# RoPE over eight slabs: one load for slabs 2 and 3, one store for slabs 4 and 5

## The chip, the cores and the metric

The kernel runs on one core of a Trainium2 chip. The metric is device time in microseconds: 162.28 us before the change (median of 3 runs, 162.27 to 162.35). The core has a vector engine (DVE), a scalar engine (ACT), a tensor engine (PE), GpSimd (POOL) and SyncE (SP), and 16 DMA engines that move data between the device's memory (DRAM in the names) and the on-chip memory of 128 partitions.

## The reference

`x` holds 16 batches of 512 positions with 1024 values each, 16 heads of 64. In each head the first 32 values and the last 32 values are rotated against each other by an angle of the position:

```python
x = x.reshape(batch, seq, num_heads, head_dim)      # 16, 512, 16, 64
x1, x2 = x[..., :half_dim], x[..., half_dim:]
cos = cos[None, :, None, :]                         # 512 x 32
sin = sin[None, :, None, :]
rotated = np.concatenate([x1 * cos - x2 * sin,
                          x1 * sin + x2 * cos], axis=-1)
```

Input and output are float32, 33.55 MB each.

## The kernel before, in words

**Slabs.** Two batches make a slab (`nb = 2`), so there are eight slabs, 0 to 7, of 4.19 MB. A slab lies in a tile of 128 partitions by 8192 floats (32 KB a partition); a partition holds 8 consecutive positions of one batch, and partitions follow each other in DRAM without gaps. Six slabs fit at a time: the pool `slabs` has six buffers, and slabs 6 and 7 reuse the buffers of slabs 0 and 1.

**Tables.** The cos and sin tables are loaded by two small transfers (line 70), cast to bfloat16 by POOL (line 89), spread over the partitions by four matmuls (line 94) and copied from there by DVE to `tab` (line 100). DVE needs `tab` before its first product.

**The work on a slab** is done in place. ACT casts the float32 values to bfloat16 into the first half of the same bytes (`cast`, line 119). DVE makes two products, with the cos table into the second half and with the sin table onto the first (line 129), and one sum of them with the 32-value halves of each head swapped (line 132). ACT casts the sum back to float32 over the slab (the write-back, line 135). Slabs 1 to 5 are done in one pass of 8192 values a partition, slabs 0, 6 and 7 in two passes of 4096.

**Order.** The loop over passes (line 123) is unrolled. ACT's program runs one pass ahead with its casts: it has the cast of the next pass before the write-back of this one. A scheduler places the instructions on each engine, so a store need not stand right behind its write-back. Each engine takes its instructions in that order and a waiting instruction holds up those behind it. SyncE issues the loads (line 61) and ACT the stores (line 137), each on a DMA queue of its own; both queues are worked off by the same 16 DMA engines. Loads 0 to 5 are issued at the start; load 6 waits for store 0 to have landed, and load 7 for store 1, since they go to the same buffers. Each transfer reports to one of eight semaphores, which are dealt out in turn, so that a transfer can also come to wait for an earlier one that uses the same semaphore.

Of the kernel before, what the change touches and what calls it, by code (L numbers as in the profile page):

```python
# [2 lines left out]

# [4 lines left out]


@with_exitstack  # L10
def kernel(
    ctx: ExitStack,
    tc: tile.TileContext,
    x: bass.AP,
    cos: bass.AP,
    sin: bass.AP,
    num_heads: int,
    out: bass.AP,
):
    nc = tc.nc  # L20
    P = nc.NUM_PARTITIONS

    batch, seq, dim = x.shape
    nh = num_heads
    hd = dim // nh
    half = hd // 2
    bf16 = mybir.dt.bfloat16
    f32 = mybir.dt.float32

    nb = 2  # L30
    slots = 6
    nslabs = batch // nb
    rpp = nb * seq // P
    W = rpp * dim
    SP = seq // rpp
    TW = rpp * half

    out_flat = out.rearrange("b s h d -> b s (h d)")

    singles = ctx.enter_context(tc.tile_pool(name="singles", bufs=1))  # L40
    slabs = ctx.enter_context(tc.tile_pool(name="slabs", bufs=slots))
    psum = ctx.enter_context(tc.tile_pool(
        name="psum", bufs=1, space=bass.MemoryType.PSUM))


    def dram(t, s, a=0, n=W):
        return bass.AP(tensor=t.tensor, offset=t.offset + s * nb * seq * dim + a,
                       ap=[[W, P], [1, n]])


    def view(t, offset, *dims):
        return dataclasses.replace(t, offset=t.offset + offset,
                                   ap=[t.ap[0], *[list(d) for d in dims]])


    slab = {}


    def load(s):
        slab[s] = slabs.tile([P, W], f32, tag="slab", name="slab")  # L60
        nc.sync.dma_start(out=slab[s], in_=dram(x, s))  # L61


    load(0)


    cos_sb = singles.tile([SP, TW], f32, tag="cos_sb")
    sin_sb = singles.tile([SP, TW], f32, tag="sin_sb")
    for t, src in ((cos_sb, cos), (sin_sb, sin)):
        nc.scalar.dma_start(out=t, in_=bass.AP(  # L70
            tensor=src.tensor, offset=src.offset, ap=[[TW, SP], [1, TW]]))

    for s in range(1, slots):
        load(s)

    pick = singles.tile([SP, 2 * P], bf16, tag="pick")
    nc.gpsimd.memset(pick, 0.0)  # L79
    for g in range(2):  # L80
        part = view(pick, g * P, (SP, P // SP), (1, SP))
        nc.gpsimd.affine_select(  # L82
            out=part, in_=part, compare_op=mybir.AluOpType.not_equal,
            fill=1.0 - 2.0 * g, base=0, pattern=[[0, P // SP], [-1, SP]],
            channel_multiplier=1)

    tab1 = singles.tile([SP, 2 * TW], bf16, tag="tab1")
    for i, t in enumerate((cos_sb, sin_sb)):
        nc.gpsimd.tensor_copy(out=view(tab1, i * TW, (1, TW)), in_=t)  # L89

    acc = psum.tile([P, 2 * rpp * hd], f32, tag="acc")
    for i in range(2):
        for h in range(2):
            nc.tensor.matmul(  # L94
                view(acc, i * rpp * hd + h * half, (hd, rpp), (1, half)),
                view(pick, i * h * P, (1, P)),
                view(tab1, i * TW, (half, rpp), (1, half)),
                start=True, stop=True)
    tab = singles.tile([P, 2 * rpp * hd], bf16, tag="tab")
    nc.vector.tensor_copy(out=tab, in_=acc)  # L100

    passes = []
    for s in range(nslabs):
        n = rpp if 1 <= s < nslabs - 2 else rpp // 2
        passes += [(s, r, n) for r in range(0, rpp, n)]


    def halves(u):
        s, r, n = u
        t = slab[s].bitcast(bf16)
        return [view(t, (2 * r + i * n) * dim, (1, n * dim)) for i in range(2)]


    def cast(u):
        s, r, n = u
        nc.scalar.copy(out=halves(u)[0], in_=view(slab[s], r * dim, (1, n * dim)))  # L119


    cast(passes[0])
    for i, u in enumerate(passes):
        s, r, n = u
        if i + 1 < len(passes):
            cast(passes[i + 1])
        lo, up = halves(u)
        for t, a in ((up, 0), (lo, rpp * hd)):
            nc.vector.tensor_mul(  # L129
                out=t, in0=lo,  # L130
                in1=view(tab, a + r * hd, (hd, n), (0, nh), (1, hd)))
        nc.vector.tensor_add(  # L132
            out=up, in0=up, in1=view(lo, half, (hd, n * nh), (-half, 2), (1, half)))

        nc.scalar.copy(out=view(slab[s], r * dim, (1, n * dim)), in_=up)  # L135
        if r + n == rpp:
            nc.scalar.dma_start(out=dram(out_flat, s), in_=slab[s])
            if s + slots < nslabs:
                load(s + slots)


# [1 line left out]
_INS = ['x', 'cos', 'sin', 'num_heads']  # L143
_OUTS = [((16, 512, 16, 64), 'float32')]

_NUMBERS = {'num_heads': 16}


# [26 lines left out]
```

## Time and profile before

| what | us |
|---|---|
| median of 3 runs | 162.28 |
| profiled execution, its own time | 162.04 |
| profiled execution, span | 160.3 |
| ACT busy | 113.3 |
| DVE busy | 108.4 |
| PE busy | 1.2 |

The span runs from the first to the last instruction of the profiled execution; its own time is 1.74 us longer. The busy times are of the span. In the lines with 40 digits every digit is the busy share of one fortieth of the span (4.0 us) in tenths, 9 for 90% or more. In the lines of queues stand packets, MB and the share of the time of all 16 DMA engines that the queue's packets took; `q1` is the loads' queue, `q10` that of the tables and the stores. In the timeline a row is start, duration, engine and line, operation and tiles, and in square brackets the idle time before it and what ended it. `ACTq` and `SPq` are the issuing of transfers by these engines. Rows of waits give the total in us, how many, and the longest.

### The profile page before, as it was taken

How to read it: one execution, taken by the hardware profiler on the slowest of the kernel's cores; microseconds unless marked ns; L12 is line 12 of the kernel's file. 1: busy time of each engine (PE TensorE's matmuls, PEld its weight loads, DVE VectorE, ACT ScalarE, POOL GpSimd, SP SyncE). 2: the span in 40 equal slices, each digit the busy share in tenths (PEclk: the TensorE clock that was granted, in tenths of full speed). 3: DMA queues.
4: the chain of work that ended last, by engine and by line, in shares of the span. 5: the costliest groups of instructions: out<-in, count | busy, mean ns of one | idle time of the engine just before them, and what ended most of it. 6: DMA issues, size and time to landing. Idle time of an engine off the chain costs nothing.

```text
span 160.3 us, 155 instructions
## 1 busy us (share of the span) xinstructions
PE 1.2 (1%) x4; PEld 0.5 (0%) x4; DVE 108.4 (68%) x34; ACT 113.3 (71%) x23; POOL 1.8 (1%) x9
## 2 busy tenths in 40 slices
PE   0001100000000000000000000000000000000000
PEld 0000000000000000000000000000000000000000
DVE  0000399999999998998999199939559499910000
ACT  3005929999949999999939995199995999280000
POOL 2000000000000000000000000000000000000000
DMA  7999999999999999999999999999999999999993
GB/s 245 417 401 409 393 450 458 401 409 491 409 393 499 417 393 466 433 409 450 450 409 401 499 409 393 499 417 393 491 417 401 466 433 409 417 483 409 401 499 147
DMA packets 2465, 67.24 MB, mean 420 GB/s; under 512 B 289, under 2 KB 417, under 8 KB 417
## 3 DMA queue, kind: packets, MB, share of 16 engines
q1 hardware_dynamic: 1152, 33.55, 49.3%
q10 hardware_dynamic: 1312, 33.69, 48.7%
q14 instruction: 1, 0.00, 0.0%
HBM read 33.69 MB, written 33.55 MB: 420 GB/s over the span
## 4 chain that ended last, share of the span: by engine, by line
DMA 50%; DVE 20%; ACT 12%; issue 6%; PE 0%; POOLq 0%; POOL 0%; DVEq 0%; ACTq 0%; SPq 0%
DMA slab<-in_x_dram 27%; DMA out_dram<-slab 16%; DVE slab L129 14%; ACT slab L135 9%; DMA cos_sb<-in_cos_dram 7%; DVE slab L132 6%; ACT slab L119 3%; DVE tab L100 1%; PE acc L94 0%; POOLq L170 0%; POOL tab L89 0%; DVEq L129 0%; SPq L61 0%; ACTq L135 0%; ACTq L119 0%
## 5 line engine op out<-in xcount | busy, mean ns | idle before, releaser
L129 DVE TENSOR_TENSOR slab<-slab,tab 128x4096 bf16<-128x4096 bf16 (+1 forms) x22 | 71.6, 3260 | 13.2 <-ACT slab L119 12.7
L119 ACT CAST slab<-slab 128x4096 bf16<-128x4096 f32 (+1 forms) x11 | 56.6, 5154 | 23.4 <-DMA slab<-in_x_dram 23.4
L135 ACT CAST slab<-slab 128x4096 f32<-128x4096 bf16 (+1 forms) x11 | 56.6, 5154 | 5.7 <-DVE slab L132 5.7
L132 DVE TENSOR_TENSOR slab<-slab 128x4096 bf16<-128x4096 bf16 (+1 forms) x11 | 35.9, 3261 | 0.3
L100 DVE CAST tab<-acc 128x1024 bf16<-128x1024 f32 x1 | 1.2, 1225 | 18.8 <-PE acc L94 18.8
L119 ACT ACT_TABLE_LOAD x1 | 1.3, 1283 | 2.0 <-issue 2.0
L94 PE MATMUL acc<-tab,pick 64*128 64x256 bf16 x4 | 1.2, 392 | 17.6 <-POOL tab L89 17.6
L82 POOL TENSOR_SCALAR_AFFINE_SELECT pick<-pick 64x128 bf16<-64x128 bf16 x2 | 0.5, 286 | 0.1
L89 POOL CAST tab<-cos_sb 64x256 bf16<-64x256 f32 x1 | 0.4, 389 | 10.7 <-DMA cos_sb<-in_cos_dram 10.7
L94 PEld LDWEIGHTS <-pick 64*128 64x128 bf16 x4 | 0.5, 112 | 17.8 <-issue 16.3
L89 POOL CAST tab<-sin_sb 64x256 bf16<-64x256 f32 x1 | 0.4, 394 | 5.0 <-DMA sin_sb<-in_sin_dram 5.0
L79 POOL MEMSET pick<- 64x256 bf16 x1 | 0.3, 304 | 0.3 <-POOLq L156 0.3
L156 POOL MEMSET const-bfloat16-1.0<- 128x1 bf16 x1 | 0.1, 106 | 0.0
L156 POOL MEMSET const-uint8-127<- 128x1 uint8 x1 | 0.1, 106 | 0.0
L156 POOL MEMSET const-float32-0.0<- 128x1 f32 x1 | 0.1, 103 | 0.2 <-issue 0.2
L156 POOL MEMSET const-float32-1.0<- 128x1 f32 x1 | 0.1, 103 | 0.0
## 6 DMA issues: line engine op xcount, KB each, us to landing
slab<-in_x_dram SPq DMA_DIRECT2D x8, 4096.0 KB, 42.6
out_dram<-slab ACTq DMA_DIRECT2D x8, 4096.0 KB, 26.0
cos_sb<-in_cos_dram ACTq DMA_DIRECT2D x1, 64.0 KB, 11.6
sin_sb<-in_sin_dram ACTq DMA_DIRECT2D x1, 64.0 KB, 16.3
```

What stands on the lines that cost most here:

```text
L79: nc.gpsimd.memset(pick, 0.0)
L82: nc.gpsimd.affine_select(out=part, in_=part, compare_op=mybir.AluOpType.not_equal, fill=1.0 - 2.0 * g, base=0, pattern=[[0, P // SP], [-1 ...
L89: nc.gpsimd.tensor_copy(out=view(tab1, i * TW, (1, TW)), in_=t)
L94: nc.tensor.matmul(view(acc, i * rpp * hd + h * half, (hd, rpp), (1, half)), view(pick, i * h * P, (1, P)), view(tab1, i * TW, (half, rpp) ...
L100: nc.vector.tensor_copy(out=tab, in_=acc)
L119: nc.scalar.copy(out=halves(u)[0], in_=view(slab[s], r * dim, (1, n * dim)))
L129: nc.vector.tensor_mul(out=t, in0=lo, in1=view(tab, a + r * hd, (hd, n), (0, nh), (1, hd)))
L132: nc.vector.tensor_add(out=up, in0=up, in1=view(lo, half, (hd, n * nh), (-half, 2), (1, half)))
L135: nc.scalar.copy(out=view(slab[s], r * dim, (1, n * dim)), in_=up)
L156: nc = _bacc.Bacc("TRN2", target_bir_lowering=False, num_devices=1)
```

## The change

Slabs 2 and 3 now lie side by side in one tile of 128 partitions by 16384 floats, and slabs 4 and 5 in another. The pool of single slabs has two buffers in place of six and a new pool `pairs` has two of double size, so the bytes are the same. Slabs 2 and 3 are loaded by one transfer, with each partition's two runs of 32 KB taken from two places 4 MB apart in DRAM; slabs 4 and 5 are still loaded by one transfer each. Slabs 4 and 5 are stored by one transfer, issued when both are done; slabs 2 and 3 are still stored by one each. Sixteen transfers remain of eighteen. Loads 6 and 7 reuse the buffers of slabs 0 and 1 as before.

```diff
-    slabs = ctx.enter_context(tc.tile_pool(name="slabs", bufs=slots))
+    slabs = ctx.enter_context(tc.tile_pool(name="slabs", bufs=2))
+    pairs = ctx.enter_context(tc.tile_pool(name="pairs", bufs=2))
...
+    def both(t, s):
+        return bass.AP(tensor=t.tensor, offset=t.offset + s * nb * seq * dim,
+                       ap=[[W, P], [nb * seq * dim, 2], [1, W]])
...
+    def place(s):
+        t = pairs.tile([P, 2 * W], f32, tag="pair", name="pair")
+        slab[s], slab[s + 1] = view(t, 0, (1, W)), view(t, W, (1, W))
+        return view(t, 0, (W, 2), (1, W))
...
-    for s in range(1, slots):
-        load(s)
-
+    load(1)
+    nc.sync.dma_start(out=place(2), in_=both(x, 2))
+    pair = place(4)
+    for s in (4, 5):
+        nc.sync.dma_start(out=slab[s], in_=dram(x, s))
...
         if r + n == rpp:
-            nc.scalar.dma_start(out=dram(out_flat, s), in_=slab[s])
-            if s + slots < nslabs:
-                load(s + slots)
+            if s == 5:
+                nc.scalar.dma_start(out=both(out_flat, 4), in_=pair)
+            elif s != 4:
+                nc.scalar.dma_start(out=dram(out_flat, s), in_=slab[s])
+            if s < 2:
+                load(s + 6)
```

On ACT the instructions keep their order but for the stores: the store of slab 0 stood behind the cast of slab 2 and now stands before it, and the merged store stands behind the cast of the first and second half of slab 6.

More of the change, by code (lines that the diff above doesn't have):

```diff
@@ L30 @@
     nb = 2
-    slots = 6
     nslabs = batch // nb
@@ L112, in halves @@
         s, r, n = u
-        t = slab[s].bitcast(bf16)
+        t = view(slab[s], 0, (1, W)).bitcast(bf16)
         return [view(t, (2 * r + i * n) * dim, (1, n * dim)) for i in range(2)]
```

## The prediction

> **What bounds the kernel now.** I read the slices of the span first, then the queues, then the stages, the chain of waits and the timeline. The page:
>
> ```profile
> span 160.3 us, 155 instructions
> DVE  0000399999999998998999199939559499910000
> ACT  3005929999949999999939995199995999280000
> DMA  7999999999999999999999999999999999999993
> q1 hardware_dynamic: 1152, 33.55, 49.3%
> q10 hardware_dynamic: 1312, 33.69, 48.7%
> ```
>
> See that both compute engines have holes and the transfers have none: every slice but the first and the last is 9. The two queues (q1 carries the loads that SP issues, q10 the stores and the two tables that ACT issues) took 49.3 + 48.7 = 98.0% of the sixteen engines' time, so 2.0% of 160.3, or 3.2 us, is idle. Is any of that in the middle? The table by stage (after the engines' busy times, the last three columns are the granted clock, the DMA share and GB/s) says no:
>
> ```profile
> 0.00:4.00 4.00, 0.00 (x0) 0.10 (x1) 0.00 (x0) 1.28 (x1) 1.04 (x7) 1.00 0.72 246
> 24.00:38.00 14.00, 0.00 (x0) 0.00 (x0) 13.95 (x6) 14.00 (x4) 0.00 (x0) 1.00 1.01 435
> 38.00:62.00 24.00, 0.00 (x0) 0.00 (x0) 23.12 (x6) 21.76 (x4) 0.00 (x0) 1.00 1.01 436
> 122.00:140.00 18.00, 0.00 (x0) 0.00 (x0) 15.72 (x8) 14.22 (x4) 0.00 (x0) 1.00 1.01 435
> 140.00:157.00 17.00, 0.00 (x0) 0.00 (x0) 0.72 (x1) 3.60 (x1) 0.00 (x0) 1.00 1.00 432
> 157.00:160.30 3.30, 0.00 (x0) 0.00 (x0) 0.00 (x0) 0.00 (x0) 0.00 (x0) 1.00 0.37 159
> ```
>
> The first 4 us miss 28% (1.1 us) and the last 3.3 us miss 63% (2.1 us): together 3.2 us, all the idle time there is. And the rate is the same with loads alone (24 to 38: 435 GB/s), loads beside stores (38 to 62: 436) and stores alone (122 to 157: 435 and 432). So the end is set by bytes: eight slabs of 4.19 MB in and eight out through one full pipe, 9.66 us for each of the sixteen (the last four stores land at 130.33, 140.00, 149.66 and 159.32 by the trace's record of landings). Who issues what when doesn't matter as long as the pipe always has something queued. The prediction is therefore a search for a moment when, after the change, both queues are empty.
>
> The rows of the timeline that the change touches, and SP's waits:
>
> ```profile
> 37.69 7.01 ACT L119 CAST slab<-slab 128x8192 bf16<-128x8192 f32 x1
> 37.81 0.35 ACTq L137 DMA_DIRECT2D out_dram<-slab  x1
> 46.94 7.02 ACT L135 CAST slab<-slab 128x8192 f32<-128x8192 bf16 x1 [2.24 <-DVE slab L132]
> 53.99 0.34 ACTq L137 DMA_DIRECT2D out_dram<-slab  x1
> 103.71 0.34 ACTq L137 DMA_DIRECT2D out_dram<-slab  x1
> 114.26 0.34 ACTq L137 DMA_DIRECT2D out_dram<-slab  x1
> 144.44 0.34 ACTq L137 DMA_DIRECT2D out_dram<-slab  x1
> ```
>
> ```profile
> SPq L61 <- DMA out_dram<-slab: 62.3, 2, 43.3
> SPq L61 <- DMA cos_sb<-in_cos_dram: 9.0, 1, 9.0
> ```
>
> These are the cast of slab 2 (37.69), the issues of stores 0 and 1 (37.81, 53.99), the write-back of slab 1, and the issues of stores 4, 5 and 7. SP's first row is loads 6 and 7 waiting for stores 0 and 1 to land; the second is load 5 waiting for the cos table, with which it shares a semaphore.
>
> **The change, part by part.**
>
> Two transfers removed. Bytes, partitions and 32 KB runs stay as they are. What a boundary between transfers costs is read where one queue runs alone: landings 9.67, 9.66 and 9.66 us apart at 432 to 435 GB/s, with no idle time in the stage. A completion write is 9 ns in the trace's packet records; two fewer on every engine is 0.02 us. The other bound is the load-only stage, where landings are 9.96 and 9.72 us apart (13.81, 23.77, 33.49), 0.30 and 0.06 over the store pitch; if all of that were boundary, two boundaries would give back 0.1 to 0.6 us. I take 0.02, because the store rows are clean of anything else, while in the first load interval the sin table is also moving. The Trainium skill, DMA: Bandwidth & Descriptors, section Anatomy of one DMA, gives every transfer (there issued by GpSimd) a fixed cost of about 2 us beside bytes over the rate; were that paid here in series, two fewer would save 4 us and end near 158.3, but the landings 9.66 us apart have no room for it.
>
> The load of slabs 2 and 3. Slab 2 can no longer be cast when its own bytes are in (33.49, landing record) but when both are. The same bytes are in front of that moment as in front of load 3's landing before, 45.67. So the cast of 2 moves from 37.69 to 45.7. The issue of store 0 stood behind that cast in ACT's program and now stands before it: it stays at 37.8. Behind the cast on ACT stand the write-back of 1, the cast of 3 and the issue of store 1; on DVE the products of 2 wait for it; on SP load 7 waits for store 1. ACT then runs back to back, a full pass every 6.92 us (46.94, 53.86, 60.78, 67.70 in the timeline): cast 2 at 45.7, write-back 1 at 52.6, cast 3 at 59.5, store 1 issued at 59.7 (5.7 us later than before), write-back 2 at 66.4, cast 4 at 73.4, store 2 at 73.5, write-back 3 at 80.3, cast 5 at 87.2, store 3 at 87.3, write-back 4 at 94.1. DVE keeps up: two products and the sum take 13.33 us (46.82 to 60.15), against 13.84 for a cast and a write-back.
>
> Does the pipe run dry here? Store 0's packets end at 59.5. A store issued into a busy pipe sends its first packet 3.6 us later (37.81 to 41.39 for store 0), so store 1 starts near 63.3 and the store queue is empty for 3.8 us. Loads 4 and 5 are queued and take the whole pipe meanwhile: cost 0. They are the cover; without them it would be 3.8 us. Loads then run 1.9 us ahead and stores 1.9 us behind (half of the 3.8). Store 1 lands near 82.5 instead of 80.4 and releases load 7, which is needed only when load 6 is through, near 100: cost 0. Load 5's wait for the cos table goes, and SP's queue issues it some 9 us sooner; the bytes in front of it last past 60, so gain 0.
>
> One store for slabs 4 and 5. The issues at 103.71 and 114.26 become one. Cast 5 ends at 94.2; DVE ends slab 5 at 107.6; its write-back runs 107.6 to 114.7 (the cast of the first half of 6, due when load 6 lands near 101.8, is over by 105.5); the store is issued at 114.7, first packet near 118.3. It stands on ACT behind the cast of 6's second half (114.6) and in front of the write-back of 6's first half (118.2), so its wait holds nothing up. When is it needed? The last packet of all ended at 158.99; four stores of 9.66 from there back give 120.3, the moment when the other twelve slabs are through. Slack 2.0 us, cover: the tails of store 3 and load 7. Cost 0.
>
> The tail. From write-back 5 by the half passes (3.60 and 2.29 us rows): casts and write-backs of 6 and 7 put store 6 at 128.9 (needed by about 136, that is 139.7 less 3.6) and store 7 at 142.8, earlier than 144.44 before since load 7 lands about 2 us earlier; needed by 145.8. Cost 0.
>
> Sharing and rate of the new shape. No row shows a transfer whose engine alternates between two places 4 MB apart. Nearest rows: loads beside stores, where every engine alternates between two tensors, at 436 GB/s (cost 0); the load-only pitch, 0.06 to 0.30 us a slab over the store pitch, which on four slabs is +0.24 to +1.2 us; on the gain side nothing below 9.66 was seen. I take 0, by the mixed row. A rule speaks against the change: the same page, Latency and other measured facts, gives 103 GB/s for partitions laid 4 MiB apart; at that rate the 16.8 MB of the two pairs would take 163 us instead of 39 and the kernel 286 us. Here the partitions stay 32 KB apart and only the two halves are 4 MB apart, so I don't expect it, and no run shown has that layout.
>
> Sum against the profiled execution: 160.3 - 0.02 = 160.3 span, 162.04 with the 1.74 that lies around it. The median shown is 162.28, 0.24 over that execution, so 162.26 there.
>
> **The rivals.**
>
> Slower, the pipe dries up at 120.3. The merged store reaches the engines after loads 0 to 7 and stores 0 to 3 are through. It decides from 2.0 us of lateness on, one for one. The pair could land later than 45.67 if store 0 shared the pipe from the end of its issue (38.2) instead of from 41.39: then 43.1 (23.77 + 2 x 9.67) plus 4.9 us, 48.0, 2.4 late, price 0.4: 162.7. For it: the slack is thin and ACT has no hole between 45.7 and 101. Against: the 41.39 is measured in the same state, and ACT's durations don't vary.
>
> Slower, the pairs' packets run at the load-only pitch or the like: +0.24 to +1.2, 162.5 to 163.5. For it: engines with no spare time, so that 1% on four slabs is already 0.4 us. Against: 435 GB/s in every mix.
>
> Faster, the boundary costs something after all: 0.1 to 0.6, 161.7 to 162.2. For it: 9.96 and 9.72 between the loads. Against: the tail stores.
>
> The change doing nothing of what it says would be a transfer split up again on its way to the queues; the built program has one instruction for each pair, and split ones would give the same 162.3 anyway.
>
> **How the numbers follow.** About 0.2% (0.3 us) is what a measurement of this kernel can tell from no change. Forecast, no change, 162.26: 0.58. Dry pipe 0.10, slower packets 0.18, other losses in a pipe that forgives nothing 0.02: slower 0.30. Cheaper boundaries: 0.12. The range 161.8 to 163.4 takes in most of the boundary gain, the dry pipe and nearly all of the packet price; the likeliest case alone is 162.1 to 162.5.
>
> **What would show it.** Right: 9 in every inner slice of the DMA row; the cast of slab 2 near 45.7; stores 0 and 1 issued near 37.8 and 59.7; the merged store near 114.7; one store queue gap near 60 with loads filling it; the last stores 9.66 us apart. Wrong: a slice under 9 near 120 (dry pipe), the pair landing clearly after 46 or a stage under 430 GB/s where a pair moves (packets), or a span shorter with the same 98% (boundaries).

## The result, and the profile after

The changed kernel takes 164.13 us (median of 22 runs, 162.01 to 165.23), the kernel before beside it 162.25 us (median of 22). The ratio is 1.0056, 95% interval 1.0036 to 1.0076. That ratio leaves out every run more than 1.5% above the fastest of its kernel, and 10 of the changed kernel's own 22 runs lie there, so its median tells more than the ratio. The kernel before keeps within 0.4 us apart from a few runs far off, the changed one spreads over 3.2 us. It is slower, and the forecast of no change was wrong.

The page of the changed kernel, its execution of 165.23 us:

```profile
span 163.4 us, 153 instructions
DVE  0000399999950999899899989999096799600000
DMA  7999999999999999999999899999999899999970
q1 hardware_dynamic: 1136, 33.55, 48.5%
q10 hardware_dynamic: 1296, 33.69, 47.9%
```

The bytes are those of before, and the DMA row is still full but for two 8s, near 92 and 129 us. The last two slices are new: 7 and 0, where before there was one 3. The span is 3.1 us longer, and nearly all transfers are over some 4 us before its end.

The rows of its timeline that answer to those of before (the cast of slab 2, the write-back of slab 1, the issues of stores 0 and 1, the merged store, stores 6 and 7):

```profile
38.08 0.35 ACTq L155 DMA_DIRECT2D out_dram<-slab  x1
45.91 7.02 ACT L134 CAST pair<-pair 128x8192 bf16<-128x8192 f32 x1 [7.86 <-DMA pair<-in_x_dram]
52.83 7.01 ACT L150 CAST slab<-slab 128x8192 f32<-128x8192 bf16 x1
59.88 0.34 ACTq L155 DMA_DIRECT2D out_dram<-slab  x1
114.96 0.39 ACTq L153 DMA_DIRECT2D out_dram<-pair  x1
131.16 0.35 ACTq L155 DMA_DIRECT2D out_dram<-slab  x1
145.33 0.34 ACTq L155 DMA_DIRECT2D out_dram<-slab  x1
```

Up to the merged store these rows are where the prediction put them, to within 0.3 us: cast 45.91 (45.7), store 1 59.88 (59.7), merged store 114.96 (114.7). Stores 6 and 7 are later than worked out, 131.16 against 128.9 and 145.33 against 142.8. That was the first thing to look at, but the next two fences show that it is not the cause. They are tables by stage (the last three columns are granted clock, DMA share and GB/s), first of the changed kernel, then of the kernel before:

```profile
75.00:97.00 22.00, 0.00 (x0) 0.00 (x0) 20.90 (x6) 22.00 (x4) 0.00 (x0) 1.00 1.01 436
97.00:109.00 12.00, 0.00 (x0) 0.00 (x0) 11.93 (x4) 9.06 (x3) 0.00 (x0) 1.00 0.98 412
142.00:158.00 16.00, 0.00 (x0) 0.00 (x0) 0.00 (x0) 3.30 (x1) 0.00 (x0) 1.00 1.01 438
158.00:163.40 5.40, 0.00 (x0) 0.00 (x0) 0.00 (x0) 0.00 (x0) 0.00 (x0) 1.00 0.06 24
```

```profile
97.00:109.00 12.00, 0.00 (x0) 0.00 (x0) 9.37 (x3) 6.58 (x3) 0.00 (x0) 1.00 1.01 434
109.00:122.00 13.00, 0.00 (x0) 0.00 (x0) 9.41 (x5) 12.25 (x3) 0.00 (x0) 1.00 0.96 413
142.00:158.00 16.00, 0.00 (x0) 0.00 (x0) 0.00 (x0) 2.41 (x1) 0.00 (x0) 1.00 0.99 428
158.00:163.40 5.40, 0.00 (x0) 0.00 (x0) 0.00 (x0) 0.00 (x0) 0.00 (x0) 1.00 0.00 0
```

From 142 to 158 us the engines are full in both: store 7 was in time. From 158 us on the changed kernel still moves something, at a share of 0.06. That can be about one engine of sixteen (1/16 = 0.0625) all the time, or many for a moment. From 97 to 109 us it moves 412 GB/s where the kernel before moves 434, at a share that is still 0.98. A full share at a lower rate would mean that the packets take longer, but in so short a stage the rate alone is only a hint: the kernel before also has a stage at 413, with its share down at 0.96. Packets have to decide both questions. This is the view of the transfers, cut to 158 to 163 us:

```profile
DMA  6000060000000060000000006000000000000000
DMA packets 20, 0.13 MB, mean 26 GB/s; under 512 B 16, under 2 KB 16, under 8 KB 16
q10 hardware_dynamic: 20, 0.13, 6.2%
```

Sixteen of these twenty packets are the 4-byte completion writes, one from each engine. The other four are 32 KB stores (0.13 MB). The trace's records of single packets go one step further. They don't name the engine, but a packet starts where the one before it on its engine ended, so the records fall into sixteen chains of 64 loads and 64 stores. Three of the four stores follow each other on one chain, from 158.65 us on, and end at 162.28. A 32 KB packet takes 1.213 us in the median of both kernels. In the kernel before none between 75 and 120 us takes over 1.25 us; in the changed one 33 do, up to 1.82 us, 7.3 us too long in all. They come in bursts near 82 and 99 to 105 us and, on that one engine, at every store from 90 to 117 us: 11 slow packets, 3.1 of the 7.3 us. Of the sixteen completion writes of the last store, fifteen lie between 158.7 and 159.3 us and one at 162.29. So most of the loss is one engine that was slowed by some 3 us while loads and stores ran beside each other, and everybody waits for it at the end.

### The profile page after: what moved, and what is told of

It is laid out like the page before. It is cut to its first block, busy times and chain, and to the rows that moved or that the text cites. A ratio compares the mean times of both kernels' runs of the same rounds, so it can differ in the third digit from the quotient of the medians.

```text
span 163.4 us, 153 instructions
## 1 busy us (share of the span) xinstructions
PE 1.2 (1%) x4; PEld 0.5 (0%) x4; DVE 108.4 (66%) x34; ACT 113.4 (69%) x23; POOL 1.8 (1%) x9
## 4 chain that ended last, share of the span: by engine, by line
DMA 66%; ACT 13%; issue 5%; DVE 4%; SPq 0%; ACTq 0%
DMA pair<-in_x_dram 27%; DMA slab<-in_x_dram 25%; DMA out_dram<-slab 14%; ACT slab L150 9%; ACT slab L134 3%; DVE slab L144 3%; DVE slab L147 1%; ACT pair L134 1%; SPq L68 0%; ACTq L150 0%; ACTq L134 0%
## 5 line engine op out<-in xcount | busy, mean ns | idle before, releaser
L134 ACT CAST slab<-slab 128x4096 bf16<-128x4096 f32 (+1 forms) x7 | 28.5, 4091 | 17.3 <-DMA slab<-in_x_dram 17.3
L144 DVE TENSOR_TENSOR slab<-slab,tab 128x4096 bf16<-128x4096 bf16 (+1 forms) x14 | 36.2, 2595 | 6.4 <-ACT slab L134 6.0
L144 DVE TENSOR_TENSOR pair<-pair,tab 128x8192 bf16<-128x8192 bf16 x8 | 35.4, 4425 | 7.4 <-ACT pair L134 7.3
L134 ACT CAST pair<-pair 128x8192 bf16<-128x8192 f32 x4 | 28.1, 7015 | 7.9 <-DMA pair<-in_x_dram 7.9
L150 ACT CAST slab<-slab 128x4096 f32<-128x4096 bf16 (+1 forms) x7 | 28.5, 4089 | 3.5 <-DVE slab L147 3.5
L150 ACT CAST pair<-pair 128x8192 f32<-128x8192 bf16 x4 | 28.1, 7016 | 1.3 <-DVE pair L147 1.3
L147 DVE TENSOR_TENSOR slab<-slab 128x4096 bf16<-128x4096 bf16 (+1 forms) x7 | 18.2, 2596 | 0.2
L147 DVE TENSOR_TENSOR pair<-pair 128x8192 bf16<-128x8192 bf16 x4 | 17.7, 4425 | 0.1
```

The lines of the kernel that those rows point to most:

```text
L144: nc.vector.tensor_mul(out=t, in0=lo, in1=view(tab, a + r * hd, (hd, n), (0, nh), (1, hd)))
L147: nc.vector.tensor_add(out=up, in0=up, in1=view(lo, half, (hd, n * nh), (-half, 2), (1, half)))
```

## The experiments

**What could slow packets long after the merged load is over?** Three theories. "Late cast": the cast of slab 2 at 45.9 us makes store 1 late, the store queue has a hole near 60 us, and after it loads and stores stand in another lag to each other, in which packets are slowed. "Two places": the merged load upsets the engines. "Merged store": the other half of the change. The first four kernels take the change apart.

The changed kernel once more:

> The changed kernel once more, as the control for the three beside it. All theories: 162 to 165 us, spread over the runs, with one or more of the sixteen DMA engines ending 1 to 3 us after the rest.

162.96 us (median of 12, 161.89 to 165.13), ratio 1.0024, interval 1.0005 to 1.0042. The spread is there again. The profiled execution of this run took 162.37 us, and its slow packets add up to 7.2 us, as many as in the execution of 165.23 us. But here the sum is spread over the engines: the last one ends 0.3 us after the median of the sixteen, there 3.4 us. In these two executions at least it is not how much is lost but whether one engine bears it that makes 162.4 or 165.2.

Only the load merged:

```diff
-            if s == 5:
-                nc.scalar.dma_start(out=both(out_flat, 4), in_=pair)
-            elif s != 4:
-                nc.scalar.dma_start(out=dram(out_flat, s), in_=slab[s])
+            nc.scalar.dma_start(out=dram(out_flat, s), in_=slab[s])
...
```

> Only the load of slabs 2 and 3 is merged; slabs 4 and 5 are stored by one transfer each. Theory 'late cast' (the cast of slab 2 moves from 37.7 to 45.7 us, the store queue has a hole near 60 us, and from then on loads and stores stand in another lag to each other, in which packets of an engine are slowed): 0.5 to 1.2% over the kernel before, packets above 1.25 us between 80 and 120 us, one engine late. Theory 'two places' (the merged load itself upsets the engines): also 0.5 to 1.2%. Theory 'merged store': 162.2 us, no change.

164.18 us, ratio 1.0109 (1.0059 to 1.0158); 79 slow packets, 10.0 us in all. The loss needs no merged store.

Only the store merged:

```diff
-    nc.sync.dma_start(out=place(2), in_=both(x, 2))
+    place(2)
     pair = place(4)
-    for s in (4, 5):
+    for s in (2, 3, 4, 5):
         nc.sync.dma_start(out=slab[s], in_=dram(x, s))
```

> Only the store of slabs 4 and 5 is merged; slabs 2 and 3 are loaded by one transfer each, the pair tiles stay. Theories 'late cast' and 'two places': 162.2 us within 0.2%, every store packet at 1.21 us. Theory 'merged store': 0.5 to 1.2% over the kernel before.

162.18 us, ratio 1.0005 (0.9996 to 1.0015), no slow packet between 75 and 120 us. The merged store and the pair tiles cost nothing, and one completion fewer brings nothing, within 0.15%. "Merged store" is out.

The timing without the merging: slab 2 is loaded in two halves around the load of slab 3, in the kernel before.

```diff
-    for s in range(1, slots):
-        load(s)
+    load(1)
+    slab[2] = slabs.tile([P, W], f32, tag="slab", name="slab")
+    H = W // 2
+    nc.sync.dma_start(out=view(slab[2], 0, (1, H)), in_=dram(x, 2, 0, H))
+    load(3)
+    nc.sync.dma_start(out=view(slab[2], H, (1, H)), in_=dram(x, 2, H, H))
+    for s in (4, 5):
+        load(s)
```

> The kernel before with no merged transfer and no pair tile, but slab 2 is loaded in two halves, one before and one after the load of slab 3, so that its cast waits until about 45.7 us as in the changed kernel. Theory 'late cast': 0.5 to 1.2% over the kernel before, with slow packets and a late engine as in the changed kernel. Theories 'two places' and 'merged store': 162.2 us within 0.2%.

163.05 us, ratio 1.0064 (1.0052 to 1.0077), with 8 slow packets (1.6 us) and one engine 1.1 us late. It speaks for "late cast", but weakly: the halves are packets of 16 KB, which no other kernel here has, and slow packets are few.

**The hole alone, and the merging without the hole.** The second set crosses the two. In the kernel before, the issue of store 1 is put behind the write-back of slab 2. The other stores are pinned to their places in the program; nothing else is meant to move:

```diff
-        nc.scalar.copy(out=view(slab[s], r * dim, (1, n * dim)), in_=up)
-        if r + n == rpp:
+        c = nc.scalar.copy(out=view(slab[s], r * dim, (1, n * dim)), in_=up)
+        if s == 2:
+            with tc.issue_after(c.ins):
+                nc.scalar.dma_start(out=dram(out_flat, 1), in_=slab[1])
+            load(7)
+        if r + n == rpp and s != 1:
...
```

> The kernel before with one thing moved: the issue of store 1 stands behind the write-back of slab 2 on ACT, at about 60.9 us in place of 54.0. No merged transfer, no pair tile, the cast of slab 2 at 37.7. Store 0's packets end at 59.5, so the store queue is empty for about 5 us as in the changed kernel, and afterwards loads end their slab 3 to 4 us ahead of the stores (changed kernel: 2.4 us ahead; kernel before: 2.5 us behind). Theory 'lag' (packets are slowed when the loads run a little ahead of the stores): 0.2 to 1.1% over the kernel before, packets above 1.25 us between 75 and 110 us. Rival 'two places' (the merged load itself): 162.2 us within 0.2%, every packet at 1.21 us.

163.13 us, ratio 1.0065 (1.0047 to 1.0084). Here are its stores 0 to 3 in the timeline, and then its stages:

```profile
37.55 0.35 ACTq L141 DMA_DIRECT2D out_dram<-slab  x1
60.05 0.34 ACTq L138 DMA_DIRECT2D out_dram<-slab  x1
67.55 0.34 ACTq L141 DMA_DIRECT2D out_dram<-slab  x1
81.89 0.34 ACTq L141 DMA_DIRECT2D out_dram<-slab  x1
```

```profile
97.00:109.00 12.00, 0.00 (x0) 0.00 (x0) 10.21 (x5) 8.79 (x2) 0.00 (x0) 1.00 0.99 421
142.00:158.00 16.00, 0.00 (x0) 0.00 (x0) 0.00 (x0) 0.00 (x0) 0.00 (x0) 1.00 1.00 432
158.00:163.40 5.40, 0.00 (x0) 0.00 (x0) 0.00 (x0) 0.00 (x0) 0.00 (x0) 1.00 0.02 6
```

One store issued 6 us late, with no byte, transfer or tile of the change, brings the same signature: 38 packets over 1.25 us (5.1 us in all, up to 1.78), a full share at 421 GB/s between 97 and 109 us, and one engine that ends late, at 159.78 us against a median of 158.78. Nothing at the end waited for that store: store 7 is issued at 141.59 us, earlier than the 144.44 of the kernel before.

Now both merged transfers, but store 0 held behind the cast of slab 2:

```diff
-            cast(passes[i + 1])
+            c = cast(passes[i + 1])
+            if passes[i + 1][0] == 2:
+                with tc.issue_after(c.ins):
+                    nc.scalar.dma_start(out=dram(out_flat, 0), in_=slab[0])
+                load(6)
...
-            elif s != 4:
+            elif s not in (0, 4):
...
```

Store 0 is issued at 43.10 us instead of 38.08. The write-back of slab 1 is pinned behind the same cast, where the changed kernel has it.

> The changed kernel with both merged transfers, but the issue of store 0 stands behind the cast of slab 2 again, at about 43.5 us in place of 38.1. The store queue then has no hole and the loads run about 8 us ahead of the stores. Theory 'lag': 162.2 to 162.6 us and hardly any slow packet, if a small lead is what hurts; as slow as the changed kernel, if any lead does. Rival 'two places': as slow as the changed kernel, 162.6 to 164.2 us.

162.03 us, ratio 0.9998 (0.9988 to 1.0008), and the runs lie within 0.5 us again. Page and stages of this kernel:

```profile
span 160.3 us, 153 instructions
DMA  7999999999999999999999999999999999999993
q1 hardware_dynamic: 1136, 33.55, 49.3%
q10 hardware_dynamic: 1296, 33.69, 48.7%
```

```profile
97.00:109.00 12.00, 0.00 (x0) 0.00 (x0) 11.93 (x4) 8.96 (x3) 0.00 (x0) 1.00 1.00 429
158.00:163.40 5.40, 0.00 (x0) 0.00 (x0) 0.00 (x0) 0.00 (x0) 0.00 (x0) 1.00 0.00 0
```

Both merged transfers are in it, and its page is that of the kernel before: a span of 160.3 us, 3 in the last slice, a share of 0.00 after 158 us. It has one slow packet. So the two merged transfers are worth nothing either way, and "two places" is out. What costs is where the stores stand against the loads.

**The lag.** Take as lag the time from the completion of load 5 to that of store 1 (medians of the sixteen completion writes in the trace; load 6 and store 2 give the same within 0.4 us). It is negative where the stores lead. A packet is the 32 KB row of one partition. One load packet and one store packet of an engine take 2.43 us together, so a lag of 2.4 us means that the loads are one row ahead. Two more kernels vary it. In the first, store 1 stands behind the cast of slab 4:

```diff
+            c = cast(passes[i + 1])
+            if passes[i + 1][0] == 4:
+                with tc.issue_after(c.ins):
+                    for d in (1, 2):
+                        nc.scalar.dma_start(out=dram(out_flat, d), in_=slab[d])
+                load(7)
...
```

> As the run before, but store 1 stands behind the cast of slab 4, issued at about 67.8 us, with store 2 right behind it: the store queue is empty for about 12 us, load 6 and store 1 then run nearly in step (lag about 0) and load 7 a few us behind store 2. Theory 'lag': between 162.2 us (if only loads that lead slow the packets) and 1% more (if running in step is worst), the slow packets between 71 and 91 us. Rival 'two places': 162.2 us within 0.2%.

162.01 us, ratio 0.9999 (0.9988 to 1.0010), no slow packet between 75 and 120 us. The expectation had its place wrong: store 1 was issued at 62.38 us and not 67.8. The cast of slab 4 before it starts only at 67.45 us, but load 4, for which that cast waits, had landed at 62.30, and the issue came right behind that. So the lag came out at 7.3 us, not 0. It is still telling: a store 2.3 us later than in the run with the hole of 5 us, and the loss is gone. A later store can be a faster kernel.

In the second, the cast of slab 3 is cut in two and store 1 put behind the second piece, for a lag near 0:

```diff
-        nc.scalar.copy(out=halves(u)[0], in_=view(slab[s], r * dim, (1, n * dim)))
+        lo = halves(u)[0]
+        for a, k in ((0, 5), (5, 3)) if s == 3 else ((0, n),):
+            c = nc.scalar.copy(out=view(lo, a * dim, (1, k * dim)),
+                               in_=view(slab[s], (r + a) * dim, (1, k * dim)))
...
+            if passes[i + 1][0] == 3:
+                with tc.issue_after(c.ins):
+                    nc.scalar.dma_start(out=dram(out_flat, 1), in_=slab[1])
+                load(7)
...
```

From there on the casts and write-backs are pinned to their order.

> The kernel before, with the cast of slab 3 in two pieces (5120 and 3072 values a partition) and the issue of store 1 behind the second, at about 58.5 us in place of 54.0; the ACT order is pinned from there on. No merged transfer. The hole of the store queue is about 2 us, so that loads and stores of the later slabs run nearly in step (lag about 0). So far, profiled executions had this summed slowing of packets between 75 and 120 us by the lag of the store behind the load: -2.5 us 0; 1.3 us 10.0; 2.1 to 2.4 us 3.9 to 9.7; 4.8 us 1.4 to 1.6; 7.3 us 0 to 0.5. If the slowing is strongest in step: 0.6 to 1.4% over the kernel before and a sum of 8 us or more. If it needs loads that lead: within 0.3%, a sum below 3 us.

162.33 us, ratio 1.0007 (0.9994 to 1.0020), a lag of -0.3 us, a sum of 2.6 us between 75 and 120 us. In time, running in step costs next to nothing. In packets it is not clean: 14 more are slow between 60 and 75 us, 3.4 us in all, where no other kernel has more than one. With them the sum is 5.9 us, more than in the run with the hole of 5 us, but it is spread: the last engine ends at 159.41 us, against 158.95 in the kernel before. So that the loads must lead for a loss shows in the time, not in the packets.

All profiled executions by lag (the sum is the time that packets of over 1.25 us between 75 and 120 us took beyond 1.213 us; lag and sum are of one execution, ratios are those given with each run):

| kernel | lag, us | sum, us | ratio, 95% interval |
|---|---|---|---|
| before | -2.5 | 0 | 1 |
| store merged alone | -2.5 | 0 | 1.0005 (0.9996 to 1.0015) |
| cast of 3 in two pieces | -0.3 | 2.6 | 1.0007 (0.9994 to 1.0020) |
| load merged alone | 1.3 | 10.0 | 1.0109 (1.0059 to 1.0158) |
| slabs 6 and 7 exchanged | 2.1 | 9.7 | 1.0069 (1.0029 to 1.0108) |
| changed kernel, second time | 2.3 | 7.2 | 1.0024 (1.0005 to 1.0042) |
| changed kernel | 2.4 | 7.3 | 1.0056 (1.0036 to 1.0076) |
| hole of 5 us, no work on slabs 4 to 7 | 2.4 | 3.9 | 1.0095 (1.0078 to 1.0111) |
| hole of 5 us | 2.5 | 5.1 | 1.0065 (1.0047 to 1.0084) |
| slab 2 loaded around slab 3 | 4.8 | 1.6 | 1.0064 (1.0052 to 1.0077) |
| hole of 5 us, stores to other rows | 4.8 | 1.4 | 1.0062 (1.0039 to 1.0085) |
| hole, store 1 behind the cast of 4 | 7.3 | 0 | 0.9999 (0.9988 to 1.0010) |
| both merged, store 0 held | 7.3 | 0.5 | 0.9998 (0.9988 to 1.0008) |

The sum is zero where stores lead by a row, largest where loads lead by about a row or less, small at two rows and all but gone at three. The time follows it only roughly. It also hangs on how evenly the sum falls on the engines, and one execution need not stand for its run: that of the kernel with no work on slabs 4 to 7 took 162.18 us, the other four 163.38 to 164.46.

**What do the packets collide with?** Three more kernels, of which two rule something out. The changed kernel with slab 7 in the place of slab 6 and the other way round:

```diff
     def dram(t, s, a=0, n=W):
+        s = {6: 7, 7: 6}.get(s, s)
```

> The changed kernel, but slab 7 is loaded, worked on and stored in the place of slab 6, and slab 6 in that of 7. Times and buffers are the same, only the places in DRAM differ: the load beside store 2 is 20 MB on and the one beside store 3 is 12 MB on from the stored slab, in place of 16 MB. If the slowing hangs on that distance: 162.2 us. If not: as the changed kernel, 162.4 to 164.2 us.

163.13 us, ratio 1.0069 (1.0029 to 1.0108), a sum of 9.7 us. The distance of 16 MB between the slab loaded and the slab stored is not what matters; other multiples of 4 MB are as bad.

The kernel of the 5 us hole with slabs 4 to 7 only loaded and stored:

```diff
-        nc.scalar.copy(out=halves(u)[0], in_=view(slab[s], r * dim, (1, n * dim)))
+        if s < 4:
+            nc.scalar.copy(out=halves(u)[0], in_=view(slab[s], r * dim, (1, n * dim)))
...
+        if s < 4:
             lo, up = halves(u)
...
```

> The kernel of the 5 us hole (store 1 behind the write-back of slab 2, no merged transfer), but slabs 4 to 7 are only loaded and stored: no cast, product, sum or write-back, so their output is x. ACT and DVE have nothing to do from about 82 us on, while the transfers keep their order and lag. If the slowed packets collide with what ACT and DVE read and write on chip: no slow packet after 85 us, 162.0 to 162.5 us. If the transfers slow each other alone: slow packets between 90 and 110 us remain, 162.6 to 163.4 us.

163.44 us, ratio 1.0095 (1.0078 to 1.0111). Its stages:

```profile
82.00:97.00 15.00, 0.00 (x0) 0.00 (x0) 0.00 (x0) 0.00 (x0) 0.00 (x0) 1.00 1.03 443
97.00:109.00 12.00, 0.00 (x0) 0.00 (x0) 0.00 (x0) 0.00 (x0) 0.00 (x0) 1.00 0.97 412
```

Every compute engine stands at 0.00 from 82 us on, and 22 of the 27 slow packets lie between 99.1 and 109.4 us, with the rate at 412 GB/s between 97 and 109 us. The loads and stores slow each other alone.

The kernel of the 5 us hole with stores 1 to 3 written to their slab's rows in another order:

```diff
+    def spread(t, s):
+        return bass.AP(tensor=t.tensor, offset=t.offset + s * nb * seq * dim,
+                       ap=[[W, P // 2], [P // 2 * W, 2], [1, W]])
...
-                nc.scalar.dma_start(out=dram(out_flat, 1), in_=slab[1])
+                nc.scalar.dma_start(out=spread(out_flat, 1), in_=slab[1])
...
```

> The kernel of the 5 us hole, but stores 1, 2 and 3 put partition p at row 64 (p mod 2) + p div 2 of their slab in DRAM instead of row p, so these rows of the output stand in another order; the on-chip side, the order of the packets and the lag are as they were. If the slowing comes from which places in DRAM a load and a store of neighbouring rows touch: the slow packets change, towards 162.1 us or clearly above 163.4 us. If it comes from the on-chip side or the queues: 162.7 to 163.4 us and slow packets where they were.

162.91 us, ratio 1.0062 (1.0039 to 1.0085). It tells little: most first packets of store 1 came one round later and the lag became 4.8 us, and the sum of 1.4 us is what the other kernel at 4.8 us has.

## Why the prediction was wrong

**Right, by its own steps.** The bound by transfers, and the bytes. Two completions fewer, put at 0.02 us: the run with the merged store alone and the run with both merged and store 0 held show no gain beyond their intervals of 0.1%. The rate of the new shape, taken as 0 beside +0.24 to +1.2: the latter run has both pairs at 162.03 us. The Trainium skill (DMA: Bandwidth & Descriptors, Anatomy of one DMA) gives a transfer issued by GpSimd a fixed cost of about 2 us; the 4 us that two of them would make if paid in series, an estimate, don't show in that run. The same page (Latency and other measured facts) gives 103 GB/s for copies whose partitions lie 4 MiB apart; with two halves 4 MB apart that run shows no such loss, at 162.03 us. The chain on ACT and DVE, the hole (first packet of store 1 at 63.57 us, worked out 63.3), the merged store in time at 114.96 us with no dry pipe at 120: all as worked out. In the tail stores 6 and 7 were 2.3 and 2.5 us later than worked out. That is the late engine again: fifteen engines had written load 7's completion by 119.32 us, the sixteenth at 123.56, and its cast starts at 124.01. The full share from 142 to 158 us shows that it did no harm in that execution.

**Wrong.** The step that failed is the price of the hole in the store queue: "Loads 4 and 5 are queued and take the whole pipe meanwhile: cost 0." They did take it, and the hole itself cost nothing. But the working went on to "Loads then run 1.9 us ahead and stores 1.9 us behind" and charged that nothing, on the premise from the first part that "Who issues what when doesn't matter as long as the pipe always has something queued." The shift was also larger than worked out, from a lag of -2.5 us to 2.4, that is 4.9 us against 3.8. The run with the hole alone gives that step its size: +0.65% (0.47 to 0.84), some 1.0 us, against 0. Behind the premise stood one row, 436 GB/s for loads beside stores, read as the rate of that mix. It was the rate of the mix at one lag, with stores 2.5 us ahead, and the trace of before shows no other.

**The rivals.** "Slower, the pairs' packets" had packets that take longer, and a price of up to 1.2 us, but named the wrong packets: those of the pairs have none over 1.25 us in the execution of 165.23 us, and the slow ones come 35 us and more after the merged load is over. "The pipe dries up" did not happen. The range ended at 163.4 us because no case in it had a loss on one engine alone. All prices were worked out for sixteen engines together, where 7.3 us of slow packets is 0.46 us each. In the execution of 165.23 us one engine ended 3.4 us after the median of the sixteen.

**Open.** Which resource the loads and stores share badly when loads lead by a row, why it shows in bursts when the streams pass from one slab to the next, and why it falls on one engine in some executions and on many in others. Work on ACT and DVE beside the transfers and the distance of 16 MB are excluded. DRAM against the on-chip side was not settled.

None of these kernels beats the kernel before: the best are the same within 0.1%, at the rate that the transfers set.

## What to carry to other kernels

In a kernel whose transfers are always busy, moving one issue by a few microseconds can still cost 1%, because it sets the lag between the load and the store stream for the rest of the run; a full share doesn't show it, and a rate by stage only hints at it, so look at how long the packets take and at whether the last ones end on all sixteen engines or on one. Merging transfers of 4 MB that are queued back to back brought nothing, and a load for two slabs makes the first of them wait for both. When a change moves many things, undo one and move one alone: here moving the issue of one store alone cost as much as the change did (0.65% against 0.56%), and in the changed kernel holding back another took the loss away.

## What the runs showed that was not expected

Packets of 32 KB that take 1.213 us took up to 1.82 us at one lag of two streams, with both queues full, and 1.21 us at another lag 5 us away. The slowing is not symmetric: a sum of 0 with stores 2.5 us ahead, 3.9 to 9.7 us with loads 2.1 to 2.5 us ahead. Two executions with equal sums (7.2 and 7.3 us) took 162.37 and 165.23 us, by whether one engine bore much of it. Delaying store 1 from 54.0 to 60.05 us cost 1.0 us; delaying it to 62.38 us cost nothing.
